# Two residual blocks with adaptive modulation on one core: engines in program order, one weight chunk per step, evacuations and attention heads as chains of tasks

## The chip, the cores and the metric

The kernel runs on one core of a Trainium2 chip. The metric is device time in microseconds (us), from the first to the last instruction of the program, as the runs give it; lower is better. Time before: 2207.31 us, the median of three runs (2190.99, 2207.31, 2212.43). TensorE (PE) multiplies, VectorE (DVE) and ScalarE (ACT) do the elementwise work, GpSimd (POOL) raises the few norm factors to their power, and SyncE (SP) issues every DMA. SBUF is the on-chip memory, PSUM the memory that PE writes.

## The reference

256 tokens of width 2048 in float32 pass four layers, and every projection is a product with a weight matrix that is used once.

```python
# first block: pooling layer, then dilated attention
hdn = rmsnorm(x, norm_a); u, gate = split(hdn @ w_in_a)                  # 2048 -> 2 x 2048
y = einsum('bsgc,gcd->bsgd', multiscale_causal_pool(u), w_grp_a) * scale_a
x = x + (y * silu(gate)) @ w_out_a
kv_in = rmsnorm(x, norm_kv); k = apply_rope(kv_in @ w_k); v = kv_in @ w_v
proj = rmsnorm(x, norm_b) @ w_in_b          # 3 groups of queries (16 heads of 128) and a gate
# 3 dilated causal windows, merged by softmax over their log-denominators
x = x + (merged * silu(gate)) @ w_out_b
x = rmsnorm(x, norm_f)
# second block: gMLP layer, then latent attention
shift, scale, gate = split(silu(c) @ ada_w[i] + ada_b[i])                # for each layer i, 2048 -> 3 x 2048
h = rms_norm(x, norm_g[i]) * (1 + scale) + shift
u, v, z = split(h @ a_w_in)                                              # 2048 -> 3 x 4096
v = layer_norm(gelu(v), a_ln_g, a_ln_b)
x = x + gate * ((gelu(u) * (tril(w_s) @ v + b_s) * silu(z)) @ a_w_out)
kv_shift, kv_scale = split(silu(c) @ kv_ada_w + kv_ada_b)                # 2048 -> 2 x 2048
# keys, values and queries through ranks of 512, 16 causal heads, gated by silu(z)
x = x + gate * (y @ b_w_out)
```

## The kernel before, in words

**Weights.** Every weight matrix is streamed once. A *chunk* is [128, 2 k-tiles, 512 columns], 512 KB of float32. SP loads it into a buffer `wraw` (L118, tag `wraw`, five buffers), ACT rounds it to a high part `wh` (L119), DVE subtracts what is left into `wl` (L125), and PE does three products per k-tile and tile of 128 tokens (L133 high by high, L134 high by low, L135 low by high): 12 matmuls of 512 columns for a chunk. There are 697 chunks. One chunk is called a *step* below. A block is 8 steps (2048 rows) or 2 steps (512 rows) that accumulate 512 output columns.

**Adaptive modulation ("ada").** The eight vectors that silu(c) makes (three for each layer of the second block, two for its keys) take 256 *parts*: a DMA of 512 KB into `araw` (L233) and one DVE instruction that multiplies and sums (L234). `araw` shares the five buffers of `wraw`. The generator `ada_all` emits a part's DMA and its DVE instruction together; `tick()` (L259) takes RATES[i] parts for each step (0.4, 0.25, 0.4, 0.4, 0.4, 0.57, 0.4, by stage), and `need()` takes what is still missing.

**Order.** The code writes each block's products, then its evacuation, then attention; a scheduler orders the instructions of each engine before the program is built, and moves the transposes of evacuations behind the products of the next chunks (DEFER = 96, L30, L194). On the chip each engine goes through its own list in order, and waits in place where something is not there yet.

**Stages by step:** pooling layer (u, ga, grp) 0 to 79; its output projection (oa) 80 to 111; keys (k) and values (v) 112 to 175; queries and gates of the dilated attention (q, gb) 176 to 303, with four heads worked at a time after each gate block; output projection (ob) 304 to 335; gMLP v (gv) to 399; u (gu), z (gz) and output projection (go), in two halves, to 591; the latent attention (cq, z, ukv, uq, o) to 696. Where a layer needs whole rows of what the one before it makes (ob3 to gv0, go13 to cq), `crossing()` interleaves the last projection with the first two of the next.

Of the kernel before, what the change touches and what calls it, by code (L numbers as in the profile page):

```python
# [10 lines left out]
F32 = mybir.dt.float32  # L11
# [9 lines left out]
T = 2  # L21
# [8 lines left out]
DEFER = 96  # L30
RATES = (0.4, 0.25, 0.4, 0.4, 0.4, 0.57, 0.4)
# [14 lines left out]

@with_exitstack
def tile_kernel(ctx: ExitStack, tc: tile.TileContext, A: dict, out: bass.AP):
    nc = tc.nc
# [7 lines left out]
    t2 = ctx.enter_context(tc.tile_pool(name="t2", bufs=9))  # L57
# [3 lines left out]
    sc_p = ctx.enter_context(tc.tile_pool(name="sc", bufs=1, space=PSUM))  # L61
# [51 lines left out]
    def whigh(W, k0, nk, n0, nn):  # L113
        """load weights and round them to their high part."""
        w = wp.tile([P, CK, NB], F32, tag="wraw", name=nm("wraw"), bufs=5)
        wh = wp.tile([P, CK, NB], F32R, tag="wh", name=nm("wh"))
        k = k0 % CK
        sp.dma_start(w[:, :nk, :nn], W[n0 // nn, k0 // CK, :, k:k + nk, :])  # L118
        act.activation(wh[:, :nk, :nn], w[:, :nk, :nn], AF.Copy)  # L119
        return w, wh, nk, nn  # L120

    def wlow(w, wh, nk, nn):
        """what the high part leaves."""
        wl = wp.tile([P, CK, NB], F32R, tag="wl", name=nm("wl"))
        dve.tensor_sub(wl[:, :nk, :nn], w[:, :nk, :nn], wh[:, :nk, :nn].bitcast(F32))  # L125
        return wh, wl

    def wsplit(*args):
        return wlow(*whigh(*args))
# [7 lines left out]
    class Stream:  # L137
        """Products of token rows (transposed, in two parts) with blocks of weights (W, n0, name).
        order: (block, first k tile, k tiles) of each step; token tile 1 runs `lag` steps behind tile 0."""

        def __init__(self, blocks, H, L, K, order, nn=NB, wk0=0, lag=0):
            self.blocks, self.H, self.L, self.K, self.order = blocks, H, L, K, order
            self.nn, self.wk0, self.lag = nn, wk0, lag
            self.ws = []
            self.ps = [[acc(nm(name)) for _ in range(T)] for _, _, name in blocks]
# [4 lines left out]
        def args(self, i):  # L150
            b, k0, nk = self.order[i]
            W, n0, _ = self.blocks[b]
            return W, self.wk0 + k0, nk, n0, self.nn

        def step(self, i):
            n = len(self.order)
            if len(self.ws) <= i < n:
                self.ws.append(wsplit(*self.args(i)))
            todo = [(i, j, t) for j in range(CK) for t in range(T)] if not self.lag else \
                   [(i, j, 0) for j in range(CK)] + [(i - self.lag, j, 1) for j in range(CK)]  # L160
            for ii, j, t in todo:
                if 0 <= ii < n and j < self.order[ii][2]:
                    b, k0, _ = self.order[ii]
                    mm3(self.ps[b][t], self.H, self.L, k0 + j, t, *self.ws[ii], j, self.nn,
                        k0 + j == 0, k0 + j == self.K - 1)
            if i < n:
                tick()

    def chunks(K, first=()):
        out, k = [], 0  # L170
        while k < K:
            n = first[len(out)] if len(out) < len(first) else min(CK, K - k)
            out.append((0, k, n))
            k += n
        return out

    def proj(W, hH, hL, K, n0, nn, name, wk0=0, lag=0, first=(), hook=None):
        """h @ W[wk0 * 128:, n0:n0 + nn] for both token tiles; hook(c, k0, nk) comes before chunk c."""
        st = Stream([(W, n0, name)], hH, hL, K, chunks(K, first), nn, wk0, lag)
        for i in range(len(st)):  # L180
            if hook:
                hook(i, *(st.order[i][1:] if i < len(st.order) else (K, 0)))
            st.step(i)
        return st.ps[0]

    def split_to(H, L, src):
        """H, L (float32r) from src (float32, SBUF or PSUM)."""
# [3 lines left out]
    def transpose_block(src, name):  # L191
        """[P, 512] SBUF -> PSUM [P, 4, P] (4 transposed blocks)."""
        pt = trp(nm(name))
        with tc.high_priority(offset=-DEFER):  # L194
            for j in range(4):
                pe.transpose(pt[:, j, :], src[:, j * P:(j + 1) * P], ident)
        return pt
# [5 lines left out]
    sc = const.tile([P, D], F32, name="silu_c")  # L203
    ada = {}

    def ada_init():
        sp.dma_start(sc, bcast_rows(A["c_2"][0], D))
        act.activation(sc, sc, AF.Silu)

    def store_row(src, dst, name):  # L210
        """[P, 16] transposed vector -> DRAM row."""
        pt = trp(nm(name))
        pe.transpose(pt[:16, 0, :], src, ident)
        row = T2(nm(name))
        dve.tensor_copy(row[:16, :P], pt[:16, 0, :])
        sp.dma_start(dst[0].rearrange("(k p) -> k p", p=P), row[:16, :P])
# [6 lines left out]

    def ada_vec(key, W, n0):
# [3 lines left out]
        bias = V(key + "_b")  # L228
        for j in range(16):
# [857 lines left out]
```

## Time and profile before

The profiled execution has a span of 2202.5 us; the median of the runs is 2207.3.

| Engine | busy us | share | instructions |
|---|---|---|---|
| PE | 2116.1 | 96% | 9646 |
| PE weight load | 1728.6 | 78% | 9646 |
| DVE | 1541.9 | 70% | 2317 |
| ACT | 1021.6 | 46% | 1395 |
| POOL | 38.7 | 2% | 29 |

538.27 MB are moved, a mean of 244 GB/s, and the mean granted clock of PE is 0.988 of full speed. Matmuls overlap in the pipeline and their ends are modelled, so PE's busy share is above the share in which it starts new work; the pace of PE is better read from the distance of starts.

### The profile page before, as it was taken

What the parts mean: (1) busy time and instruction counts of PE and PEld (TensorE: products, weight loads), DVE (VectorE), ACT (ScalarE), POOL (GpSimd) and SP (SyncE); (2) the same over time, 40 slices, a digit from 0 to 9 for tenths busy, and PEclk for the clock granted to TensorE, in tenths of its full rate; (3) what the DMA queues carried; (4) which work ended last, traced back from release to release, by engine and by line L of the source; (5) the groups of instructions that cost most, each with busy time, mean ns of one, the idle gap of its engine ahead of it and who ended that gap; (6) DMA issues with size and microseconds to landing.
All of it is one profiled execution on the core that took longest, in us unless ns stands there. A gap on an engine that the chain in (4) does not pass through costs nothing.

```text
span 2202.5 us, 26845 instructions
## 1 busy us (share of the span) xinstructions
PE 2116.1 (96%) x9646; PEld 1728.6 (78%) x9646; DVE 1541.9 (70%) x2317; ACT 1021.6 (46%) x1395; POOL 38.7 (2%) x29
## 2 busy tenths in 40 slices
PE   8999999999999999999999999989999899999999
PEld 6877777887878787877887778777888677878877
DVE  6566677755777777776777877777887678565654
ACT  6434444443444545444544334433444346765642
POOL 0000000000000000000000000000000000010000
PEclk9999999999999999999999999999999999999999
DMA  8767776777757575767688888889988875563344
GB/s 323 258 230 269 238 256 246 258 253 239 266 187 266 183 256 187 253 236 261 199 298 282 273 272 285 274 301 328 320 318 278 285 269 182 165 220 114 126 162 162
DMA packets 159781, 538.27 MB, mean 244 GB/s; under 512 B 17792, under 2 KB 22944, under 8 KB 159136
## 3 DMA queue, kind: packets, MB, share of 16 engines
q1 hardware_dynamic: 159648, 536.56, 71.2%
q8 instruction: 75, 1.23, 0.2%
q14 instruction: 58, 0.48, 0.1%
HBM read 525.99 MB, written 10.50 MB: 244 GB/s over the span
## 4 chain that ended last, share of the span: by engine, by line
PE 39%; DMA 33%; DVE 15%; issue 9%; ACT 1%; SPq 0%; POOL 0%; DVEq 0%; POOLq 0%; ACTq 0%
DMA araw<-in_ada_w 18%; DVE wl L125 9%; DMA araw<-in_kv_ada_w 7%; DMA wraw<-in_a_w_in 3%; PE q L135 2%; PE q L134 2%; PE q L133 2%; DVE araw L234 2%; DMA wraw<-in_a_w_out 1%; PE a1sc L484 1%; PE o L134 1%; PE o L135 1%; PE o L133 1%; DMA xb<-in_x 1%; PE go L135 1%
## 5 line engine op out<-in xcount | busy, mean ns | idle before, releaser
L119 ACT ACTIVATE wh<-wraw 128x1024 fp32r<-128x1024 f32 (+2 forms) x697 | 734.6, 1055 | 977.4 <-DMA wraw<-in_a_w_in 175.0
L125 DVE TENSOR_TENSOR wl<-wraw,wh 128x1024 fp32r<-128x1024 f32 (+2 forms) x697 | 834.5, 1213 | 196.6 <-ACT wh L119 194.2
L234 DVE CUSTOM_DVE_ANT_0 araw<-araw,silu_c,vec 128x1024 f32<-128x1024 f32 x128 | 164.2, 1283 | 175.1 <-DMA araw<-in_ada_w 141.7
L134 PE MATMUL q<-wl,hbH 128*128 128x512 f32 x384 | 153.7, 400 | 3.5 <-DVE wl L125 3.5
L135 PE MATMUL q<-wh,hbL 128*128 128x512 f32 x384 | 154.2, 401 | 0.0
L133 PE MATMUL q<-wh,hbH 128*128 128x512 f32 x384 | 152.3, 397 | 0.0
L135 PE MATMUL go<-wh,gyL 128*128 128x512 f32 x256 | 103.7, 405 | 8.4 <-DVE gyL L189 8.4
L134 PE MATMUL gu<-wl,hgH 128*128 128x512 f32 x256 | 102.5, 400 | 7.3 <-DVE wl L125 7.2
L133 PE MATMUL go<-wh,gyH 128*128 128x512 f32 x256 | 102.1, 399 | 5.1 <-ACT gyH L188 5.1
L134 PE MATMUL gz<-wl,hgH 128*128 128x512 f32 x256 | 102.1, 399 | 2.7 <-DVE wl L125 2.7
L133 PE MATMUL gu<-wh,hgH 128*128 128x512 f32 x256 | 101.9, 398 | 1.3 <-ACT wh L119 1.3
L134 PE MATMUL gv<-wl,hgH 128*128 128x512 f32 x256 | 100.7, 393 | 2.4 <-DVE wl L125 2.4
L134 PE MATMUL go<-wl,gyH 128*128 128x512 f32 x256 | 102.9, 402 | 0.0
L135 PE MATMUL gz<-wh,hgL 128*128 128x512 f32 x256 | 102.0, 399 | 0.0
L135 PE MATMUL gu<-wh,hgL 128*128 128x512 f32 x256 | 101.6, 397 | 0.0
L133 PE MATMUL gz<-wh,hgH 128*128 128x512 f32 x256 | 101.5, 397 | 0.0
L133 PE MATMUL gv<-wh,hgH 128*128 128x512 f32 x256 | 100.5, 392 | 0.6 <-ACT hgH L532 0.6
L135 PE MATMUL gv<-wh,hgL 128*128 128x512 f32 x256 | 100.2, 391 | 0.0
L134 PEld LDWEIGHTS q<-wl,hbH 128*128 128x128 f32 x384 | 72.5, 189 | 20.0 <-DVE wl L125 4.8
L135 PEld LDWEIGHTS q<-wh,hbL 128*128 128x128 f32 x384 | 72.6, 189 | 15.2
L133 PEld LDWEIGHTS q<-wh,hbH 128*128 128x128 f32 x384 | 72.5, 189 | 13.5
L234 DVE CUSTOM_DVE_ANT_0 araw<-araw,silu_c,ada_ga 128x1024 f32<-128x1024 f32 x32 | 41.1, 1284 | 51.9 <-DMA araw<-in_ada_w 51.9
(367 smaller groups left out, 4464.9 us busy)
## 6 DMA issues: line engine op xcount, KB each, us to landing
araw<-in_ada_w SPq DMA_DIRECT2D x192, 512.0 KB, 4.9
wraw<-in_a_w_in SPq DMA_DIRECT2D x192, 512.0 KB, 5.0
wraw<-in_w_in_b SPq DMA_DIRECT2D x128, 512.0 KB, 4.5
araw<-in_kv_ada_w SPq DMA_DIRECT2D x64, 512.0 KB, 4.6
wraw<-in_a_w_out SPq DMA_DIRECT2D x64, 512.0 KB, 5.6
wraw<-in_w_in_a SPq DMA_DIRECT2D x63, 512.0 KB, 4.9
wraw<-in_b_w_in SPq DMA_DIRECT2D x40, 512.0 KB, 3.6
wraw<-in_w_out_a SPq DMA_DIRECT2D x32, 512.0 KB, 4.7
```

The costliest lines, as they stand in the source:

```text
L119: act.activation(wh[:, :nk, :nn], w[:, :nk, :nn], AF.Copy)
L125: dve.tensor_sub(wl[:, :nk, :nn], w[:, :nk, :nn], wh[:, :nk, :nn].bitcast(F32))
L133: pe.matmul(p[:, :nn], hH[:, k, ts], wh[:, j, :nn], start=start, stop=False)
L134: pe.matmul(p[:, :nn], hH[:, k, ts], wl[:, j, :nn], start=False, stop=False)
L135: pe.matmul(p[:, :nn], hL[:, k, ts], wh[:, j, :nn], start=False, stop=stop)
L234: dve.tensor_tensor_reduce(out=w, in0=w, in1=sc[:, hs], scale=1.0, scalar=d[:, j:j + 1] if half else bias[:, j:j + 1], op0=OP.mult, op1=OP ...
L484: pe.matmul(psc[:, g * nk:(g + 1) * nk], qT[g][:, hh, t * P:(t + 1) * P], kT[:, h, :nk], start=True, stop=True)
```

## The change

The scheduler is switched off (`tc.manual_schedule()`), and each engine's instructions stand in the order in which the code emits them. A list PLAN holds all 697 chunks in the order of use. Each step calls `begin()`, then its 12 matmuls, then `end()`. `begin()` emits, in this order: `high` on ACT of the chunk four steps ahead (AHEAD); the tasks that are due in this step; one head that is ready, from `headq`; one PSUM fill from `trq` (transposes, mixing products), which is used one step later; `low` on DVE of the chunk four ahead; and the load of the chunk seven ahead. `end()` starts parts of ada by the stage's rate; the DMA is issued there, the DVE instruction follows two steps later. The evacuations, norms and heads are chains of such tasks with fixed distances in steps. The rates are 0.5 from the first gate block, 0.3 (oa), 0.5 (k), 0.7 (v), 0.5 and then 0.15, 0.15, 0 and 0.2 (attention), 0.3 and 0 (ob), 0.78 (gv), 0.5 (gu), 0.68 (gz), 0.74 (go), 0 after that. The order of blocks in the first attention changes (L1: gb2 and gb3 come last, heads are spread over the query blocks), as does that of the second one (L3); the first two blocks of `w_out_b` and of `w_out2` run as a pair. Sixteen heads of the first attention scale their output on ACT (32 instructions) and multiply by the gate in 8 DVE instructions of 128x512, where 32 DVE instructions did both. `t2` has 11 buffers for 9. The work of PE, the bytes and the five `wraw` buffers stay.

```diff
-DEFER = 96
-RATES = (0.4, 0.25, 0.4, 0.4, 0.4, 0.57, 0.4)
+AHEAD = 4
+FETCH = 3
...
+    ctx.enter_context(tc.manual_schedule())
...
-    t2 = ctx.enter_context(tc.tile_pool(name="t2", bufs=9))
+    t2 = ctx.enter_context(tc.tile_pool(name="t2", bufs=11))
...
+    L1 = [(0, 0), (1, 0), (2, 0), (3, 0), (0, 1), (1, 1), (2, 1), (3, 1), (0, 2), (1, 2), (2, 2),
+          (0, 3), (1, 3), (2, 3), (3, 2), (3, 3)]
...
+    def through(d, name, fill, use):
+
+        def go():
+            pt = trp(nm(name))
+            fill(pt)
+            after(1, lambda: use(pt))
+        if d:
+            after(d, lambda: trq.append(go))
+        else:
+            trq.append(go)
...
+        while clk["hi"] < min(n, c + clk["ahead"] + 1) and len(lows) < 2:
+            high(clk["hi"])
+            lows.append(clk["hi"])
+            clk["hi"] += 1
+        for fn in tasks.pop(clk["s"], ()):
+            fn()
+        if headq and headq[0][0] <= clk["s"] and ready.issuperset(headq[0][1]) and clk["s"] >= clk["head"] + headq[0][2]:
+            clk["head"] = clk["s"]
+            headq.pop(0)[3]()
+        if trq:
+            trq.pop(0)()
+        for i in lows:
+            low(i)
+        m = 0
+        while clk["dma"] < min(n, c + clk["ahead"] + 1 + FETCH) and m < 2:
+            fetch(clk["dma"])
+            clk["dma"] += 1
+            m += 1
+
+    def end():
+        clk["due"] += clk["rate"]
+        while clk["due"] >= 1:
+            clk["due"] -= 1
+            next(ada_gen, None)
...
-        for j in range(16):
-            for half in range(2):
-                hs = slice(half * 1024, (half + 1) * 1024)
-                w = wp.tile([P, CK * NB], F32, tag="wraw", name=nm("araw"), bufs=5)
-                sp.dma_start(w, W[n0 // P + j, half])
-                dve.tensor_tensor_reduce(out=w, in0=w, in1=sc[:, hs], scale=1.0,
+
+        def part(j, half):
+            w = wp.tile([P, CK * NB], F32, tag="wraw", name=nm("araw"), bufs=5)
+            sp.dma_start(w, W[n0 // P + j, half])
+
+            def mul():
+                dve.tensor_tensor_reduce(out=w, in0=w, in1=sc[:, half * 1024:(half + 1) * 1024], scale=1.0,
+                                         scalar=d[:, j:j + 1] if half else bias[:, j:j + 1],
+                                         op0=OP.mult, op1=OP.add, accum_out=d[:, j:j + 1])
...
+            after(2, mul)
...
+        def first():
+            score(0)
+            after(1, lambda: top(0))
+            after(2, lambda: expo(0))
+            when(2, [(("q", g, hq), 1) for g in range(3)], second)
+
+        def second():
+            score(1)
+            after_each(1, lambda: top(1), lambda: (expo(1), add(0)), lambda: add(1))
+            through(4, "a1et", etr, ecopy)
+        headq.append((clk["s"] + d, [(("q", g, hq), 0) for g in range(3)], 3, first))
...
+                clk["rate"] = (0.15, 0.15, 0.0, 0.2)[hq]
...
+    clk["rate"] = 0.78
...
+        clk["rate"] = 0.5
...
+        clk["rate"] = 0.68
...
+        clk["rate"] = 0.74
```

How this moves instructions is seen in three places. The first is SP's list in the gv stage, which holds nothing but loads; `wraw` is a chunk of weights, `araw` a part of ada, and the numbers tell tiles apart. Before:

```order
L233 DMA araw_8597<-in_kv_ada_w 128x1024
L118 DMA wraw_8606<-in_a_w_in 128x1024
L118 DMA wraw_8624<-in_a_w_in 128x1024
L233 DMA araw_8642<-in_kv_ada_w 128x1024
L118 DMA wraw_8645<-in_a_w_in 128x1024
L233 DMA araw_8663<-in_kv_ada_w 128x1024
```

and of the change:

```order
L230 DMA wraw_8662<-in_a_w_in 128x1024
L407 DMA araw_8676<-in_kv_ada_w 128x1024
L230 DMA wraw_8682<-in_a_w_in 128x1024
L407 DMA araw_8696<-in_kv_ada_w 128x1024
L230 DMA wraw_8703<-in_a_w_in 128x1024
L407 DMA araw_8717<-in_kv_ada_w 128x1024
L230 DMA wraw_8724<-in_a_w_in 128x1024
```

Before, one or two chunks stand between two parts; now parts and chunks mostly alternate. The second place is DVE's list for the same loads: `wl` reads a chunk of weights and L234 (L410 in the change) a part, and each of these reads frees one of the five buffers. Before:

```order
L125 TENSOR_TENSOR wl_8565<-wraw_8561,wh_8562 128x1024
L234 ISA araw_8597,ada_kvsh<-araw_8597,silu_c,vec 128x1024
L234 ISA ada_kvsh 128x1
L125 TENSOR_TENSOR wl_8583<-wraw_8579,wh_8580 128x1024
L125 TENSOR_TENSOR wl_8610<-wraw_8606,wh_8607 128x1024
L234 ISA araw_8642,ada_kvsh<-araw_8642,silu_c,ada_kvsh 128x1024
```

and of the change:

```order
L252 TENSOR_TENSOR wl_8680<-wraw_8622,wh_8678 128x1024
L410 ISA araw_8676,ada_kvsh<-araw_8676,silu_c,vec 128x1024
L410 ISA ada_kvsh 128x1
L252 TENSOR_TENSOR wl_8701<-wraw_8643,wh_8698 128x1024
L410 ISA araw_8696,ada_kvsh<-araw_8696,silu_c,ada_kvsh 128x1024
L410 ISA ada_kvsh 128x1
L252 TENSOR_TENSOR wl_8722<-wraw_8662,wh_8719 128x1024
L410 ISA araw_8717,ada_kvsh<-araw_8717,silu_c,vec 128x1024
```

Before, three reads stand between the read that frees a buffer for `araw_8642` (that of `wraw_8561`, after which four loads are left unread) and its own; now two stand between that for `araw_8717` (of `wraw_8643`) and its own. The third place is PE's list where the first attention starts its first head; `a1sc` are the scores of a head, L484 (L674 in the change), with 128 keys for the first tile of tokens and 256 for the second. Before:

```order
L135 MATMUL gb_833_4402<-wh_4539,hbL 128x512
L484 MATMUL a1sc_4560<-kT,qT_4015 128x128
L484 MATMUL a1sc_4560<-kT,qT_4195 128x128
L484 MATMUL a1sc_4560<-kT,qT_4376 128x128
L133 MATMUL q_1_901_4718<-wh_4721,hbH 128x512
L134 MATMUL q_1_901_4718<-wl_4724,hbH 128x512
L135 MATMUL q_1_901_4718<-wh_4721,hbL 128x512
L133 MATMUL q_1_902_4719<-wh_4721,hbH 128x512
L484 MATMUL a1sc_4572<-kT,qT_4015 128x256
```

and of the change:

```order
L295 MATMUL gb_869_4488<-wh_4455,hbL 128x512
L674 MATMUL a1sc_4578<-kT,qT_4107 128x128
L674 MATMUL a1sc_4578<-kT,qT_4290 128x128
L674 MATMUL a1sc_4578<-kT,qT_4473 128x128
L293 MATMUL gb_868_4487<-wh_4474,hbH 128x512
L294 MATMUL gb_868_4487<-wl_4483,hbH 128x512
L295 MATMUL gb_868_4487<-wh_4474,hbL 128x512
```

Before, the scores of the second tile come four products after those of the first; now they come 24 products after them, two steps.

## Rows read from the trace of the kernel before

**Rows 1.** Page, part 1: engine, busy us, share of the span, instructions.

```profile
PE 2116.1 (96%) x9646; PEld 1728.6 (78%) x9646; DVE 1541.9 (70%) x2317; ACT 1021.6 (46%) x1395; POOL 38.7 (2%) x29
```

**Rows 2.** Page, part 4: chain that ended last, by engine and by line.

```profile
PE 39%; DMA 33%; DVE 15%; issue 9%; ACT 1%; SPq 0%; POOL 0%; DVEq 0%; POOLq 0%; ACTq 0%
DMA araw<-in_ada_w 18%; DVE wl L125 9%; DMA araw<-in_kv_ada_w 7%; DMA wraw<-in_a_w_in 3%; PE q L135 2%; PE q L134 2%; PE q L133 2%; DVE araw L234 2%; DMA wraw<-in_a_w_out 1%; PE a1sc L484 1%; PE o L134 1%; PE o L135 1%; PE o L133 1%; DMA xb<-in_x 1%; PE go L135 1%
```

**Rows 3.** Windows by stretch, B to F: us, busy us per engine, clock, DMA.

```profile
57.00:539.00 482.00, 464.99 (x2065) 381.10 (x2064) 315.82 (x382) 206.34 (x235) 1.07 (x1) 0.98 0.73 250
539.00:972.20 433.20, 419.18 (x2001) 342.87 (x2000) 321.09 (x565) 200.51 (x257) 2.01 (x1) 0.99 0.67 228
972.20:1113.70 141.50, 137.46 (x614) 112.44 (x614) 101.10 (x144) 72.58 (x110) 3.11 (x4) 0.99 0.73 244
1113.70:1788.50 674.80, 647.63 (x2833) 527.30 (x2833) 508.29 (x653) 273.59 (x295) 1.59 (x1) 0.98 0.85 293
1788.50:2202.50 414.00, 397.36 (x1930) 324.79 (x1928) 259.31 (x531) 231.15 (x447) 29.99 (x17) 0.99 0.50 166
```

**Rows 4.** Windows of L133 alone (four matmuls a step), stretches C and E.

```profile
539.00:972.20 433.20, 203.17 (x512) 96.61 (x512) 0.99 0.67 228
1113.70:1788.50 674.80, 355.22 (x896) 170.42 (x897) 0.98 0.85 293
```

**Rows 5.** Timeline, PE, dense products: start us, duration us; first and last of 42.

```profile
591.64 0.39 PE L134 MATMUL gb<-wl,hbH 128*128 128x512 f32 x1
...
600.95 0.39 PE L133 MATMUL gb<-wh,hbH 128*128 128x512 f32 x1
```

**Rows 6.** Waits of DVE in stretch E: us in total, times, longest.

```profile
DVE araw L234 <- DMA araw<-in_ada_w: 80.8, 50, 4.6
DVE araw L234 <- DMA araw<-in_kv_ada_w: 44.4, 26, 3.1
DVE wl L125 <- ACT wh L119: 27.1, 23, 5.2
```

**Rows 7.** Waits of DVE in stretch C.

```profile
DVE araw L234 <- DMA araw<-in_ada_w: 44.3, 21, 3.9
DVE wl L125 <- ACT wh L119: 31.2, 33, 2.5
DVE araw L234 <- DMA araw<-in_kv_ada_w: 20.6, 9, 3.7
```

**Rows 8.** Waits of DVE in stretch B.

```profile
DVE araw L234 <- DMA araw<-in_ada_w: 129.2, 47, 4.7
```

**Rows 9.** Tile araw, whole program: from issue to landing.

```profile
DMA to landing us min/median/max: 3.3/4.8/9.4
```

**Rows 10.** Timeline in gz, DVE and SP's queue; idle before in brackets.

```profile
1418.92 1.28 DVE L234 CUSTOM_DVE_ANT_0 araw<-araw,silu_c,vec 128x1024 f32<-128x1024 f32 x1 [3.55 <-DMA araw<-in_ada_w]
1420.13 2.36 DVE L125 TENSOR_TENSOR wl<-wraw,wh 128x1024 fp32r<-128x1024 f32 x2
1420.24 0.33 SPq L233 DMA_DIRECT2D araw<-in_ada_w  x1
...
1423.79 1.28 DVE L234 CUSTOM_DVE_ANT_0 araw<-araw,silu_c,ada_sh 128x1024 f32<-128x1024 f32 x1 [1.31 <-DMA araw<-in_ada_w]
```

**Rows 11.** Timeline, PE in the first attention: heads between products.

```profile
622.80 0.59 PE L484 MATMUL a1sc<-kT,qT 128*128 128x256 f32 x2
623.23 0.27 PE L448 MATMUL a1et<-ident,a1sm 128*128 128x128 f32 x1
623.34 0.27 PE L449 MATMUL a1et<-ident,a1sm 128*128 128x128 f32 x1
623.45 1.03 PE L484 MATMUL a1sc<-kT,qT 128*128 128x256 f32 x4
```

**Rows 12.** Waits of PE in stretch C.

```profile
PE a1sc L484 <- DVE a1sms L426: 12.8, 4, 5.5
```

**Rows 13.** Page, part 5, one of the costliest groups: busy us, mean ns, idle before.

```profile
L119 ACT ACTIVATE wh<-wraw 128x1024 fp32r<-128x1024 f32 (+2 forms) x697 | 734.6, 1055 | 977.4 <-DMA wraw<-in_a_w_in 175.0
```

More of the change, by code (lines that the diff above doesn't have):

```diff
@@ L128, in wsplit, with after, when @@
-    def wsplit(*args):
-        return wlow(*whigh(*args))
+    clk = {"s": 0, "c": 0, "dma": 0, "hi": 0, "ahead": AHEAD, "rate": 0.0, "due": 0.0, "head": 0}
+    tasks = {}
+    raws, parts = {}, {}
+    def after(d, fn):
+        tasks.setdefault(clk["s"] + d, []).append(fn)
+    trq, headq = [], []
+    ready = set()
+    def when(d, keys, fn):
+        def go():
+            if ready.issuperset(keys):
+                fn()
+            else:
+                after(1, go)
+        after(d, go)
@@ L391, in rope_evac @@
+    after(4, inv_b)
+    after(6, rope_inv)
     def rope_evac(p, t, tab, name):
@@ L402, in rope_evac, with rope_block, go, out @@
         return a
-    pace["rate"] = RATES[2]
+    def rope_block(ps, name, key, dst):
+        for t in range(T):
+            def go(t=t):
+                a = rope_evac(ps[t], t, rope, name)
+                def out(pt):
+                    act.activation(dst(t), pt, AF.Copy)
+                    ready.add((key, t))
+                tr_then(2, a, name + "tr", out)
+            after(1 + t, go)
+    clk["rate"] = 0.5
     kT = B16(F32, "kT")
@@ L573, in crossing @@
             if i == last + s1.lag:
[L574 to L582 removed]
+                fin(0, s1.ps[0])
+        fin(1, s1.ps[1])
+        clk["ahead"] = AHEAD
     x3d = dram.tile([S, D], F32, name="x3d")
@@ new lines, in tile_kernel, with ob_gmod @@
+    obs = []
+    def ob_gmod():
+        need("sh0", "sc0")
+        gm0.append(gmod("sc0", "norm_g0"))
+    after(12, ob_gmod)
+    after(11, lambda: obs.append(Ob(0, 0)))
+    after(14, lambda: obs.append(Ob(1, 0)))
+    proj2(["ob0", "ob1"], mH, mL, 12, lambda b, ps: obs[b].whole(ps))
+    clk["rate"] = 0.3
+    ob = Ob(2, 4)
+    ob.whole(proj(mH, mL, KT, "ob2"))
+    clk["rate"] = 0.0
+    ob = Ob(3, 6)
+    hH, hL = B16(F32R, "hgH"), B16(F32R, "hgL")
+    vg = [big.tile([P, GW], F32, tag="b16", name=f"vg{t}") for t in range(T)]
@@ L959, in tile_kernel @@
[L959 to L981 removed]
+            as_.append(a)
@@ new lines, in ntr, with out, rtr, fill @@
+        def ntr(t):
+            def out(pt):
+                act.activation(qs_[hq][0][:, :, t * P:(t + 1) * P], pt, AF.Copy, scale=V("g_qn"))
+                ready.add(("qn", hq, t))
+            tr_then(0, ns[t], "q2tr", out)
+        def rtr(t):
+            def fill(pr):
+                for h in range(4):
+                    pe.transpose(pr[:64, h, :], as_[t][:, h * 64:(h + 1) * 64], ident)
+            def out(pr):
+                act.activation(qs_[hq][1][:, :, t * P:(t + 1) * P], pr[:64], AF.Copy)
+                ready.add(("qr", hq, t))
+            through(0, "q2rt", fill, out)
@@ new lines, in tile_kernel @@
+    need("ga1")
+    o2s = [O2(0, 10), O2(1, 12)]
+    proj2(["o20", "o21"], oH, oL, 12, lambda b, ps: o2s[b].whole(ps))
+    o2 = O2(2, 4)
+    o2.whole(proj(oH, oL, KT, "o22"))
+    o2 = O2(3, 4)
+    clk["ahead"] = LAG
+    s = Stream(["o23"], oH, oL, KT, chunks(KT), lag=LAG)
+    for i in range(len(s)):
+        s.step(i)
+        if i == len(s.order) - 1:
+            o2.evac(s.ps[0][0], 0)
+    assert not trq
+    for k in sorted(tasks):
+        clk["s"] = k
+        for fn in tasks.pop(k):
+            fn()
@@ L984, in _constants @@
+    o2.evac(s.ps[0][1], 1)
+    assert not tasks and clk["c"] == len(PLAN)
 def _constants():
```

1307 lines of the change are left out of this document (776 added, 531 removed).

## The prediction, made before the change was run

> **What bounds the kernel now.** I read the page from the outside in. PE is busy for 96% of the span [rows 1], but the chain that ended last has only 39% of PE in it: DMA holds 33%, most of it landings of `araw` (18% and 7%), and DVE 15% [rows 2]. Busy PE isn't PE at its pace, since ends are modelled. The pace shows in a dense stretch: 42 products of 512 columns start within 9.31 us [rows 5], 0.227 apart, so a step of 12 is 2.72 us. I then cut the span where the steps 16, 176, 304, 352 and 576 begin, into stretches B to F [rows 3] (A, the first 57 us, is left alone: its first chunk and its x bound it in both).
>
> E holds 896 / 4 = 224 steps [rows 4], which at 2.72 us are 609 us; its other 145 PE instructions, at about 0.12 us each (transposes start 0.11 apart [rows 11]), add 17. PE needs 627 us there and the stretch takes 674.8 [rows 3]. What fills it is DVE: 508.3 us busy [rows 3], 125.2 us waiting for parts of ada to land (76 waits) and 27.1 us for ACT [rows 6], together 661, and what is left (14) goes to small waits. Nothing of weight waits for PE. So from gv to go DVE sets the time, and three quarters of the time in which it doesn't compute (125 of 166.5 us) are landings. C is the same: 321.1 busy, 64.9 landings, 31.2 for ACT [rows 3, 7] are 417 of 433.2. In B 129.2 us are landings [rows 8].
>
> Why a landing is waited for is seen in gz [rows 10]. DVE's product at 1418.92 frees a buffer, SP issues the next part at 1420.24, two `wl` take 2.36 us, and then the next product stands at the head of DVE's queue until 1423.79. The landing took 3.6 us there and takes 4.8 as a median [rows 9]. Everything behind waits too: `wl`, evacuations, and in the attention the score masks, for which PE waited 12.8 us in 4 waits [rows 12].
>
> **What the change does to this.** PE's work and the bytes stay, so the terms are waits. Five buffers serve chunks and parts in both versions, and a part's load can start only when at most four loads are unread. So the DVE work between the read that frees its buffer and its own read is fixed by DVE's and SP's lists. I counted it for every part in both, at DVE's pace in the trace (some 1.2 us for a `wl` and for a part, start to start [rows 10]). In the lists shown above it is a part and two `wl`, 3.5 us, before, and a part and one `wl`, 2.3 us, in the change. Call the *shortfall* 4.8 us less that work, where it is positive. The number of parts moves as well, by the rates.
>
> - **E, gv to go.** Parts 126 before, 146 after (rates 0.78, 0.5, 0.68, 0.74 for 0.57). With under 3.8 us of work between: 83 of 126 before, 128 of 146 after. Shortfalls sum to 165 us before, of which DVE really waited 125.2 [rows 6], that is 0.76 (one wait covers part of the next landing). After, they sum to 288; 0.76 of that is 219 us. DVE then needs 508.3 + 20 x 1.28 (the added parts [rows 10], 25.6) + 219 = 753 us, +78, with the waits for ACT and the norm's loads taken as gone. Lower bound: waits per part stay at 125.2 / 126 = 0.99 us, 146 x 0.99 = 145, in all 679, +4. Upper bound: every shortfall is waited for, 822, +147. I take +62, nearer the first figure, since the count of close parts is in the lists and only the landing can give: a longer stretch carries its bytes at a lower rate (293 GB/s now [rows 3]), which shortens landings a little. What covers nothing here: the `low` four steps ahead is a stock of 11 us, spent once.
> - **C, first attention.** Parts 52 to 23; shortfall 102 to 32, so landings 64.9 to 21 us. DVE: 321.1 - 29 x 1.28 + 21 = 305 and some 30 for ACT, no longer the bound. PE is: 128 x 2.72 = 348, plus 16 heads at some 2.9 us (6 scores at 0.215, 6 at half of it, 3 transposes at 0.11, 6 products at 0.11 [rows 11]), 46, plus 128 transposes, 15: 410. I keep 5 us of PE's 14 of idle time for scores that wait for the softmax [rows 12]. 415, -18. Bounds: 0 to -23. The 16 heads' scaling on ACT is hidden, ACT is busy for 201 of 433 us [rows 3]; without that cover 32 instructions of 128 columns cost between an eighth and a half of 1.055 us each [rows 13], 4 to 17 us.
> - **B, pooling to values.** Parts 60 to 78 (rates 0.5, 0.3, 0.5, 0.7), 18 x 1.28 = 23 us more work; shortfall 145 to 153, landings 129.2 to 136. DVE 315.8 + 23 + 136 = 475, with small waits about the 482 of now; PE needs 160 x 2.72 + 145 x 0.12 = 452. 0, bounds -20 and +30.
> - **D, ob and the crossing.** The chain through the norm (reduce, power on POOL, row on PE, splits) stands as it was; pairing ob0 and ob1 moves its waits. 0, bounds -6 and +6.
> - **F, rest.** 7 parts leave, heads are spread over 11 blocks, POOL makes one factor of 16 columns for two of 8. PE shows 414.0 - 397.4 = 16.6 us of idle [rows 3]; I take it as gained, -16. Bounds: 0, and -30 for idle that modelled ends hide. A head's scores, tops and copies now stand at fixed places in PE's and DVE's lists; if a predecessor is late, products queue behind it.
>
> Sum: 2202.5 + 62 - 18 + 0 + 0 - 16 = 2230.5 us for a profiled execution. The median of the runs stands 4.8 above the profiled one, so 2235.
>
> **The rivals.** *Landings are hidden (faster).* Parts and chunks alternate and each is issued at a fixed place, so fewer loads may be in flight at once; a landing alone takes 3.3 us, the shortest row [rows 9]. At 3.3 E's shortfalls are 117, 0.76 of it 89; DVE needs 623 us there, PE 627, so E takes some 639 (-36). B gains its 20, C and F as above: 2202.5 - 36 - 20 - 18 - 16 = 2112, or 2117 as a median. It decides from a landing of about 3.8 us downwards (where DVE's sum in E falls to the 675 of now). Against it: the median is 4.8 with fewer parts. [...]
>
> *Waits per part stay as they are.* One wait in a close pair covers the other's landing, so closeness costs nothing more: E at +4, the rest as forecast, 2202.5 + 4 - 18 - 16 = 2172.5, median 2177. For it: 0.76 is already under 1. Against it: waits in B, where more parts are close (44 of 61 under 2.6 us), are 129.2 / 60 = 2.2 us per part [rows 8], not 0.99.
>
> *The fixed order of PE adds stalls (slower still).* Some 260 fills stand at fixed places, and the scheduler's freedom to have put them behind what was ready is gone. At 0.1 us each this is 26 us on top of my sum, 2261. Against it: a fill is used a step after it is written, and its input is made one or two steps (2.7 to 5.4 us) before.
>
> *The change doesn't do what it says.* The lists show the order as described; under 0.02, and I leave it out.
>
> **How the numbers follow.** My case 0.50, with a range of its own from 2195 to 2262 (E between +22 and +89); fixed-order stalls 0.17; waits per part unchanged 0.20; landings hidden 0.13. About 1% (22 us) is what a measurement of this kernel can tell from no change, so faster is below 2185 and slower above 2229. My case puts 0.30 of its 0.50 above 2229 and the rest between; stalls put 0.15 above; unchanged waits put 0.14 below 2185 and 0.06 within; hidden landings all below. Faster 0.27, same 0.28, slower 0.45. The range leaves out the lower part of the hidden landings and the upper part of the stalls, about 0.1 on either side: 2135 to 2275.
>
> **What would show it.** Right: in the profile after, E (from the third gv block to the third block of go's second half) is longer than 674.8 us with DVE waiting some 200 us for `araw` there, and landings near 4.8; C is near 415 us with under 30 us of such waits, and PE's dense starts there; F is near 398. E near 640 with landings under 4 us would make the first rival right, E near 680 with about 1 us of wait per part the second. Many short waits of PE for `tr` and `sc` tiles, or a granted clock well under 0.988 over a stretch, would make the third right. My step most likely to fail is that the landing keeps its median: the shortfall counts every tenth of it 128 times in E.

## The result, and the profile after

The changed kernel takes 2311.98 us (median of four runs, 2305.68 to 2315.03) where the kernel before takes 2204.38 beside it: 1.0485 times as long, 95% interval 1.0444 to 1.0527. Slower was forecast, at 2235 us with a range up to 2275; the loss is about four times as large as forecast and lies outside the range.

The page of the profile after, part 1 (engine, busy us, share of the span, instructions), answers to [rows 1]:

```profile
PE 2144.7 (93%) x9646; PEld 1742.9 (75%) x9646; DVE 1554.8 (67%) x2253; ACT 1016.0 (44%) x1382; POOL 31.0 (1%) x25
```

PE runs the same 9646 instructions; the span of the profiled execution grew from 2202.5 to 2313.3 us. The same cuts as in [rows 3], at the starts of steps 16, 176, 304, 352 and 576 (windows of the kernel after: us, busy us of PE, weight load, DVE, ACT, POOL, clock, DMA share, GB/s):

```profile
55.80:530.10 474.30, 462.79 (x2080) 379.43 (x2081) 337.90 (x420) 207.83 (x239) 0.70 (x1) 1.00 0.81 272
530.10:962.50 432.40, 417.33 (x1995) 346.81 (x1994) 287.70 (x465) 207.31 (x289) 0.00 (x0) 0.99 0.58 190
962.50:1116.60 154.10, 140.37 (x622) 113.67 (x621) 100.84 (x142) 73.36 (x111) 4.12 (x5) 0.97 0.66 223
1116.60:1879.60 763.00, 672.60 (x2834) 536.52 (x2833) 536.63 (x684) 272.64 (x295) 0.70 (x1) 0.96 0.81 274
1879.60:2313.30 433.70, 405.60 (x1929) 329.59 (x1927) 256.78 (x504) 222.09 (x400) 24.57 (x13) 0.97 0.46 151
```

E (gv to go) is the loss: 763.0 after 674.8. C (first attention) stayed at 432.4, D (ob and its crossing) grew by 12.6 and F (second crossing and the rest) by 19.7. In E the clock was granted at 0.96 for 0.98 and the memory carried its bytes at a lower rate than before, 274 GB/s for 293. DVE's busy time grew by 28 us, of which the 20 added parts are 26. What grew most is DVE's waiting for parts (waits of DVE in E after: us in total, times, longest), which answers to [rows 6]:

```profile
DVE araw L410 <- DMA araw<-in_ada_w: 130.8, 78, 5.3
DVE araw L410 <- DMA araw<-in_kv_ada_w: 70.6, 45, 3.3
DVE gyL L356 <- ACT gyH L355: 9.4, 9, 2.8
DVE wl L252 <- ACT wh L242: 7.4, 8, 2.1
```

These are 201.4 us of landings in 123 waits, where it was 125.2 in 76 before. So the 88 us more in E are 28 of DVE's work and 76 of landings, less 16 that DVE waits less for all else (25 us for 41). The pattern repeats for whole blocks (timeline of the kernel after in gu, DVE and SP's queue: start us, us, operation, idle before in brackets):

```profile
1297.71 2.35 DVE L252 TENSOR_TENSOR wl<-wraw,wh 128x1024 fp32r<-128x1024 f32 x2
1297.83 0.33 SPq L407 DMA_DIRECT2D araw<-in_kv_ada_w  x1
...
1302.45 1.28 DVE L410 CUSTOM_DVE_ANT_0 araw<-araw,silu_c,ada_kvsc 128x1024 f32<-128x1024 f32 x1 [2.38 <-DMA araw<-in_kv_ada_w]
...
1303.66 2.35 DVE L252 TENSOR_TENSOR wl<-wraw,wh 128x1024 fp32r<-128x1024 f32 x2
1303.77 0.33 SPq L407 DMA_DIRECT2D araw<-in_kv_ada_w  x1
...
1308.15 1.28 DVE L410 CUSTOM_DVE_ANT_0 araw<-araw,silu_c,vec 128x1024 f32<-128x1024 f32 x1 [2.14 <-DMA araw<-in_kv_ada_w]
```

A product frees the buffer, the next part is issued 0.1 us later, two `wl` cover 2.4 us of a landing of 4.6, and DVE stands. A landing of 4.6 us is the median of all parts (tile `araw` after, beside [rows 9]; it is also that of E alone):

```profile
DMA to landing us min/median/max: 3.3/4.6/9.7
```

PE, which waited 27 us in E before, now waits 90 us there, for what is queued behind that. The longest waits of PE in E, before:

```profile
PE go L135 <- DVE gyL L189: 8.4, 4, 3.0
PE gu L134 <- DVE wl L125: 7.2, 5, 2.1
```

and after:

```profile
PE gytr L369 <- DVE gz L1085: 27.1, 7, 8.8
PE gu L294 <- DVE wl L252: 22.6, 15, 5.4
PE go L294 <- DVE wl L252: 15.5, 11, 3.1
PE gv L294 <- DVE wl L252: 12.5, 14, 2.0
```

In C the landings fell as forecast, from 64.9 to 18.6 us, and still PE waited there (waits of PE in C after, beside [rows 12]):

```profile
PE qrtr L369 <- DVE qr L617: 9.4, 3, 6.4
PE a1sc L674 <- ACT qT L627: 2.4, 2, 1.2
PE a1sc L674 <- DVE a1s L682: 2.1, 2, 1.5
```

Where in C this was is seen if it is cut once more, at step 200 (window of steps 176 to 199 of the kernel after, and the waits of DVE in it):

```profile
530.10:613.60 83.50, 74.11 (x325) 60.54 (x324) 58.05 (x80) 32.41 (x35) 0.00 (x0) 0.94 0.74 245
```

```profile
DVE araw L410 <- DMA araw<-in_ada_w: 18.6, 8, 3.4
DVE wl L252 <- ACT wh L242: 6.5, 4, 1.8
```

All of C's landings are waited for in its first 24 steps, where parts are still started at the rate of 0.5. There DVE's busy time and its waits (58.1 + 18.6 + 6.5 us) fill the 83.5 us: DVE is the bound, and PE's whole wait for `qr` lies there.

### The profile page after: what moved, and what is told of

Same layout as the page of the kernel before. It is cut to its first block, busy times and chain, and to the rows that moved or that the text cites. A ratio compares the mean times of both kernels' runs of the same rounds, so it can differ in the third digit from the quotient of the medians.

```text
span 2313.3 us, 26922 instructions
## 1 busy us (share of the span) xinstructions
PE 2144.7 (93%) x9646; PEld 1742.9 (75%) x9646; DVE 1554.8 (67%) x2253; ACT 1016.0 (44%) x1382; POOL 31.0 (1%) x25
## 5 line engine op out<-in xcount | busy, mean ns | idle before, releaser
L410 DVE CUSTOM_DVE_ANT_0 araw<-araw,silu_c,vec 128x1024 f32<-128x1024 f32 x128 | 164.3, 1283 | 175.5 <-DMA araw<-in_ada_w 131.0
L294 PEld LDWEIGHTS gu<-wl,hgH 128*128 128x128 f32 x256 | 49.3, 193 | 39.9 <-DVE wl L252 30.1
```

The lines of the kernel that those rows point to most:

```text
L294: pe.matmul(p[:, :nn], hH[:, k, ts], wl[:, j, :nn], start=False, stop=False)
L410: dve.tensor_tensor_reduce(out=w, in0=w, in1=sc[:, half * 1024:(half + 1) * 1024], scale=1.0, scalar=d[:, j:j + 1] if half else bias[:, j: ...
```

## The experiments

The theory from the prediction is called theory A in the expectations below: parts of ada stand too near to their own loads on DVE. Its rivals are PE's fixed order (theory B), and too few buffers whatever is read first (theory C). The columns A to F of the table are something else, the stretches of the text above, cut at the same steps in every kernel, in us of the profiled execution. The last column is the median of four or more executions for the first two rows and the kernel with 4 steps, and a single execution for the others; where an interval is given below, there were four. B and C repeat within 0.1 us in kernels whose edits leave them alone, but E lies between 662.5 and 668.9 for 4 steps with edits that lie outside it, so differences of a few us in E are not read:

| Kernel | A | B | C | D | E | F | whole, us |
|---|---|---|---|---|---|---|---|
| before | 57.0 | 482.0 | 433.2 | 141.5 | 674.8 | 414.0 | 2204 |
| after (product 2 steps after the load) | 55.8 | 474.3 | 432.4 | 154.1 | 763.0 | 433.7 | 2312 |
| 3 steps | 57.9 | 457.7 | 418.2 | 153.0 | 677.3 | 433.9 | 2200 |
| 4 steps | 55.9 | 457.8 | 416.5 | 152.6 | 666.6 | 436.0 | 2185 |
| after, no parts | 56.2 | 457.7 | 417.6 | 153.0 | 633.1 | 433.8 | 2153 |
| before, no parts | 56.3 | 461.7 | 414.9 | 142.6 | 633.7 | 406.1 | 2117 |
| after, even rates | 58.1 | 473.5 | 433.1 | 153.6 | 722.9 | 433.7 | 2277 |
| 4 steps, even rates | 56.2 | 457.7 | 422.0 | 153.0 | 664.7 | 432.5 | 2188 |
| 2 steps, 7 buffers | 56.9 | 457.6 | 419.1 | 156.9 | 646.7 | 438.0 | 2177 |
| 4 steps, rows behind products | 57.9 | 457.7 | 416.4 | 150.8 | 662.5 | 432.4 | 2179 |
| 4 steps, low parts later | 59.3 | 457.7 | 416.5 | 152.0 | 664.0 | 433.3 | 2185 |
| 4 steps, pieces in three steps | 56.3 | 457.7 | 416.5 | 149.7 | 668.9 | 419.2 | 2170 |
| the same, statistics earlier | 55.8 | 457.7 | 416.4 | 145.2 | 667.7 | 417.9 | 2163 |

### One line: when a part is read

```diff
-            after(2, mul)
+            after(4, mul)
```

> The changed kernel with one line altered: the DVE instruction of a part of ada comes 4 steps after its load is issued instead of 2. By the lists of the built program the DVE work between the read that frees a part's buffer and the part's own read grows from a mean of 2.9 us to 5.8 in the gv to go stretch (148 parts), and for the chunks of weights it shrinks from 7.8 to 6.7. Theory A (the landings set that stretch): DVE's waits for araw there fall from 201 us to under 50, the stretch from 763 us to 655 to 690, and the whole from 2312 to about 2210. Theory B (PE's fixed order sets it: transposes and fills that stand ahead of products): the waits fall, but the stretch stays above 740 and the whole above 2285. Theory C (five buffers are short whatever is read first): the wait moves to the chunks, ACT waits for wraw some 100 us more, and the stretch stays near 730, the whole near 2280.

Measured: 2184.7 us, 0.9904 of the kernel before (0.9876 to 0.9932), 127 us less than the change. Theory A forecast about 2210. In the whole program DVE's waits for parts are down to nothing (waits before the tile `araw`, whole program, kernel with 4 steps):

```profile
  DMA araw<-in_ada_w: 2.3, 3
  DMA araw<-in_kv_ada_w: 0.3, 1
```

though a landing's median is longer there, 5.1 us, than in the kernels before and after, 4.8 and 4.6:

```profile
DMA to landing us min/median/max: 3.4/5.1/9.6
```

E is 666.6, with 148 parts, and C 416.5 (window of E with 4 steps):

```profile
1082.70:1749.30 666.60, 643.38 (x2834) 527.21 (x2833) 532.04 (x679) 271.63 (x294) 1.56 (x1) 0.99 0.89 311
```

DVE now waits for ACT's `wh` instead (82.9 us in E, where it was 7.4), but that is time it has to spare: PE's waits for `wl` in E fell from 52 to 15 us. ACT's waits for chunks to land, 288 us in E of the changed kernel, are 277, so the wait didn't move to the chunks: theory C falls as the cause of what this edit gained. Theory B falls for E, since PE's list kept its order. PE's waits in E for `gytr` fell from 27.1 to 1.5 us: they were what the parts had made late.

> The same with 3 steps instead of 2 or 4. Mean DVE work between is 4.3 us in the gv to go stretch, the sum of shortfalls (4.8 us less that work, where positive) 115 us there after 288 at 2 steps and 10 at 4. Theory A: DVE's waits for araw there fall from 201 to about 80 us, the stretch to some 680 to 700 us, the whole to about 2230, between the changed kernel and the one with 4 steps. Theory B: no change, above 2285.

Measured: 2199.82 us, E 677.3, waits for parts 75.0 there (waits of DVE in E, 3 steps):

```profile
DVE araw L410 <- DMA araw<-in_ada_w: 46.4, 40, 4.6
DVE araw L410 <- DMA araw<-in_kv_ada_w: 28.6, 35, 2.2
```

The sums of shortfalls, 288, 115 and 10 us for 2, 3 and 4 steps, gave waits of 201, 75 and about 3. The waits were forecast well (80), the time less so (2200 for 2230): once PE leads again, 75 us of DVE's waits cost only 11 of E. That the stock of finished chunks takes up the rest is my reading; no run varies that stock alone.

### Without any parts

```diff
-            w = wp.tile([P, CK * NB], F32, tag="wraw", name=nm("araw"), bufs=5)
-            sp.dma_start(w, W[n0 // P + j, half])
...
-                dve.tensor_tensor_reduce(out=w, in0=w, in1=sc[:, half * 1024:(half + 1) * 1024], scale=1.0,
...
+                    dve.tensor_copy(d, bias)
```

(in the changed kernel; the same is left out of the kernel before)

> The changed kernel without the adaptive modulation's loads and products: each of the eight vectors is a copy of its bias, nothing else is left out. So no part is loaded, waited for or computed, and what is left is the order itself. Theory A: gv to go falls from 763 to 640 to 665 us (PE needs 627), pooling to values from 474 to about 455, the first attention from 432 to about 425, the whole to about 2185. Theory B: gv to go stays above 720, the whole above 2260.

> The kernel before without the adaptive modulation's loads and products, vectors are copies of their biases. Theory A: gv to go falls from 675 to about 635 us, the first attention from 433 to about 412, pooling to values from 482 to about 456, the whole from 2202 to about 2113. What the changed kernel without it takes above this one is the price of the fixed order by itself: from the traces 35 to 70 us, in the two crossings, the attentions and the transposes. Theory B: the difference is 100 us or more, all of the loss.

Measured: 2153.18 us, below the 2185 expected, and 2117.06 us. In E both are PE's pace and equal (windows of E without parts, kernel after and kernel before):

```profile
1084.50:1717.60 633.10, 633.10 (x2834) 524.58 (x2833) 363.58 (x393) 273.08 (x295) 0.70 (x1) 1.00 0.64 206
```

```profile
1075.50:1709.20 633.70, 633.68 (x2833) 523.57 (x2832) 363.23 (x397) 275.63 (x295) 1.60 (x1) 1.00 0.64 206
```

So the new order by itself costs nothing in E, gains 4 us in B, and costs 36 us in all: 3 in C, 10 in D and 28 in F, where the crossings are.

### Number or nearness

```diff
-    clk["rate"] = 0.78
+    clk["rate"] = 0.58
...
-                clk["rate"] = (0.15, 0.15, 0.0, 0.2)[hq]
+                clk["rate"] = (0.4, 0.4, 0.1, 0.2)[hq]
```

> The changed kernel with the parts of ada spread about as before: a rate of 0.58 in all of gv to go (129 parts there by the lists, for 146) and 0.4, 0.4, 0.1, 0.2 in the first attention (42 parts for 23); the product still comes 2 steps after the load is issued. It tells the number of parts in the last stretch from their nearness. Theory A (nearness, each near part costs DVE its wait): shortfalls in gv to go fall from 288 to 241 us, of which 0.70 was waited in the changed kernel, so 168 us of waits after 201; with 17 fewer parts of 1.28 us the stretch is some 705 to 715 us after 763, the first attention rises from 432 to about 440, the whole is about 2265. Rival (the 20 added parts are the loss): the stretch returns to about 680 and the whole to about 2235.

Measured: 2276.58 us, E 722.9, above both readings, nearest to theory A's. With 129 parts in E, where the kernel before has 126, E is 48 us above it; as the order costs nothing in E without parts, that is nearness. The 17 parts more that the change has there are the other 40, half of them DVE's work (17 x 1.28 = 22 us) and half waits (201.4 - 181.6 = 20 us). The waits behind them (waits of DVE in E, even rates) are 181.6 us, not the 168 expected:

```profile
DVE araw L410 <- DMA araw<-in_ada_w: 136.1, 77, 6.4
DVE araw L410 <- DMA araw<-in_kv_ada_w: 45.5, 30, 2.8
```

> The kernel with 4 steps and the even rates of the earlier run (129 parts in gv to go, 42 in the first attention). That stretch takes 666.6 us with 148 parts and 633.1 without any, so 33.5 us still hang on the parts. If each costs the same, 0.23 us, the stretch falls by only 4 us, to 662, and the whole to about 2181. If it is DVE's or DMA's load near its limit (278 GB/s and 80% of DVE's time there), the last parts cost most: about 645 to 650, and the first attention, with 18 more parts, stays within 4 us of 416.5; the whole about 2168.

Measured: 2187.84 us, E 664.7 for 666.6, C 422.0 for 416.5: once parts are read in time their number hardly counts, and moving them gives nothing. The second reading of that expectation fell (the memory carries 311 GB/s in E with 4 steps, not the 278 named there), and the whole was not the 2181 of the first either.

### Buffers

```diff
-AHEAD = 4
+AHEAD = 3
...
-    wp = ctx.enter_context(tc.tile_pool(name="wp", bufs=5))
+    wp = ctx.enter_context(tc.tile_pool(name="wp", bufs=4))
...
-        w = wp.tile([P, CK * NB], F32, tag="wraw", name=nm("wraw"), bufs=5)
+        w = wp.tile([P, CK * NB], F32, tag="wraw", name=nm("wraw"), bufs=7)
```

(and the same 7 for `araw`)

> The changed kernel with its product 2 steps after the load as it is, but chunks rounded three steps ahead instead of four, and the memory so freed given to the loads: 7 buffers for chunks and parts instead of 5, 4 instead of 5 for high and low parts. DVE work between is 5.8 us for parts in gv to go, 10.9 for chunks (7.8 in the changed kernel, 6.7 with the product at 4 steps). Theory A (a landing needs buffers or distance, either will do): waits for araw go below 20 us, gv to go to 660 or less, the whole to about 2180 or less. If the stock of finished chunks matters more, the whole stays above 2215.

Measured: 2176.82 us, E 646.7, waits for parts 20.3 us there. Distance in DVE's list or buffers, either will do for the parts, and buffers give the chunks their distance as well. ACT's waits for chunks to land in E show it, with 4 steps and five buffers:

```profile
ACT wh L242 <- DMA wraw<-in_a_w_in: 203.0, 111, 7.4
ACT wh L242 <- DMA wraw<-in_a_w_out: 73.8, 33, 5.1
```

and with 2 steps and seven:

```profile
ACT wh L242 <- DMA wraw<-in_a_w_out: 11.4, 4, 5.6
ACT wh L242 <- DMA wraw<-in_a_w_in: 9.8, 2, 8.3
```

So theory C holds for most of what 4 steps leave in E: 666.6 became 646.7, with 633.1 for no parts at all.

### The crossings

In the changed kernel the step in which the crossing turns over takes 15.0 us in both, where the kernel before has 8.3 and 7.0; and the steps 591 to 599 of the second take 2.7 to 8.6 us where before all take 2.7.

```diff
-            if i == n0 + 1:
-                rbs.append(stats(0, pb[:, 0:P]))
-                evac_tr(0)
             s0.step(i)
+        rbs.append(stats(0, pb[:, 0:P]))
+        evac_tr(0)
```

(and the second tile's behind the first step of the next layer)

> The kernel with 4 steps, and in both crossings PE's two instructions that need the norm of a token tile (the row of factors and the transposes) stand behind the next products instead of ahead of them, and DVE's statistics with them. If PE's place for them is what made the crossing's longest step 15.0 us (7.0 to 8.3 before), that step falls to about 9 in both crossings, the stretches with ob and with the rest lose some 5 to 6 us each, the whole goes from 2185 to about 2174. If the short stock of chunks (two steps ahead in a crossing, four elsewhere) made it, nothing changes by more than 2 us.

Measured: 2179.43 us. The long step falls to 10.0 and 9.8, but the two after it rise, in the first crossing from 4.3 and 3.5 to 6.3 and 5.3: D gains 1.8, F 3.6. The place of PE's instructions was mostly not the cause.

```diff
+            if late:
+                after(2, lows)
+            else:
+                lows()
```

> The kernel with 4 steps, and in both crossings the four joint pieces of the split input (and the four of the keys' input) make their low part one step later than their high part, so that DVE doesn't wait for ACT in between. In the second crossing the steps 591 to 598 take 3.2 to 5.9 us, 38 in all for 8, where the kernel before takes 2.7 each; DVE has there some 2.8 us of work and 1.05 of waits for ACT a step. If these waits are the loss, the steps fall to about 2.9 and the last stretch loses some 8 us, the first crossing some 3, the whole goes to about 2174. If it is DVE's work, the steps stay above 3.4 and the whole above 2181.

Measured: 2184.58 us, the steps 591 to 598 still take 3.3 to 4.5 us each (31 us in all with 4 steps alone, not 38). So the loss was not DVE's waits for the high part, but not the sum of work on DVE either, which was busy for 22.5 of 30.2 us there. The timeline of this kernel shows a ring (DVE and ACT in the second crossing, without the low part `h2L` that stands between):

```profile
1811.14 0.75 DVE L786 TENSOR_TENSOR hx<-z,inv_row 128x256 f32<-128x256 f32 x2
1811.92 0.91 ACT L790 ACTIVATE h2H<-hx,ada_sh 128x256 fp32r<-128x256 f32 x2 [1.96 <-DVE hx L786]
1812.74 1.04 ACT L242 ACTIVATE wh<-wraw 128x1024 fp32r<-128x1024 f32 x1
1813.82 1.22 DVE L252 TENSOR_TENSOR wl<-wraw,wh 128x1024 fp32r<-128x1024 f32 x1 [1.14 <-ACT wh L242]
1814.96 1.41 DVE L786 TENSOR_TENSOR hx<-zk,inv_row 128x256 f32<-128x256 f32 x4
```

From `hx` to `hx` 3.82 us: ACT rounds the chunk only behind the high part, that waits for `hx`, and `hx` stands behind the chunk's `wl`. Neither engine is full, and each waits for the other once a step.

```diff
+            if late:
+                after_each(1, highs, lows)
```

> The kernel with 4 steps, and the late pieces of the crossings go in three steps: the product with the row of factors, a step later the high part (behind the rounding of a chunk in ACT's list), another step later the low part. With only the low part moved the steps 591 to 598 stayed at 3.2 to 4.5 us. If they are set by a ring of the two lists (hx on DVE 0.75 to 0.9 us until ACT can start, high part 0.9, rounding of the chunk 1.06, wl 1.14, then the next hx, about 3.8 us a step), then this breaks it: the steps fall to about 2.8, the last stretch from 436 to about 427, the first crossing loses 2 to 3, the whole goes from 2185 to about 2175. If it is the sum of work on one engine, the steps stay above 3.4 and the whole above 2181.

Measured: 2169.99 us. Steps 591 to 598 take 2.7 us each, step 599 4.4 for 8.6, F 419.2 after 436.0, D 149.7 after 152.6: the ring was the loss in these steps, and more of it than expected. They give back 14 us; 2 of the 17 in F lie in step 576, which the edit doesn't touch. The first two edits of this section together:

> The last two together on the kernel with 4 steps. If the two losses lie in different steps they add: some 20 to 22 us, to about 2163 us, 0.982 of the kernel before. If one hides behind the other, about 2172.

Measured: 2178.69 us, 0.9887 (0.9862 to 0.9912). They don't add, since the low parts alone gave nothing.

> The kernel with 4 steps and the crossings' pieces in three steps, and in both crossings DVE's statistics of the first token tile stand straight behind its evacuation, ahead of the next chunk's wl, while PE's rows and transposes stand behind the products that follow. In the changed kernel these statistics stood for 2 us behind a wl that waited for ACT. If that place is what is left of the crossing's long step, the first three steps of the crossing go from 23.7 us to about 19 in each, the whole from 2170 to about 2160. If the chain through the norm sets them whatever the order (as the rows behind the products gave nothing), they stay at 22 to 24 and the whole at 2166 to 2172.

Measured: 2162.59 us. The long step is 7.2 and 7.7 us, the two after it 6.5 and 5.1, and 6.3 and 6.3: the first three steps go from 23.3 and 23.7 to 18.8 and 20.3, D from 149.7 to 145.2, F only from 419.2 to 417.9, where a fourth step takes 3.6. So in the first crossing the place of the statistics, behind a `wl` that waits for ACT, was worth nearly what was expected. This edit moves PE's rows as well; in the first kernel of the next section, which has the rows, the pieces and the even rates, D is 148.7, so some 3.5 of the 4.5 us are the statistics. F is 4 us above the kernel before, which has 7 parts there, and 12 above that kernel without parts: this remainder is open.

### Versions that beat both

> 4 steps, even rates, the rows behind the products, and the pieces of the crossings in three steps. Gains of its parts if they add: 10 us from the pieces, 5 from the rows, 4 to 17 from the rates, on 2185 us: 2153 to 2166, 0.977 to 0.983 of the kernel before. If the two edits in the crossings hide each other, 2165 to 2175.

Measured: 2168.0 us, 0.9831 (0.9804 to 0.9857). Its D of 148.7 and F of 422.3 stand beside 149.7 and 419.2 with the pieces alone, and its C is 422.0 for 416.5: the even rates gave nothing, the rows next to nothing.

> The crossings' pieces in three steps, the product 3 steps after the load, and chunks three steps ahead with 7 buffers for the loads. With four steps and 5 buffers gv to go takes 667 to 669 us, 34 above the kernel without parts. If those 34 us are loads that come late because five buffers hold too few (ACT waits for wraw), the stretch falls to about 642, the crossings lose 2 to 3 us each with the smaller stock, and the whole is about 2150, 0.975 of the kernel before. If they are the memory's rate (311 GB/s there), the stretch stays above 655 and the whole at about 2165.

Measured: 2157.85 us, 0.9797 (0.9755 to 0.9838), E 641.9. So 25 to 27 of the 34 to 36 us were late loads for want of buffers, and not the memory, which carried 323 GB/s there and 311 with 4 steps and five buffers (window of E):

```profile
1086.50:1728.40 641.90, 636.70 (x2835) 526.43 (x2834) 533.31 (x680) 273.87 (x295) 1.62 (x1) 0.99 0.91 323
```

F is 429.2 there and 419.2 with five buffers, D 153.9 and 149.7. The likely reason is the smaller stock of finished chunks (three steps for four), which costs more than expected in the crossings; the stock and the buffers were not run apart.

> The last two together. If both hold, about 2142 us; if only the buffers do, about 2150.

Measured, in a single execution: 2151.68 us, near its second reading. E is 640.8, D 149.6 and F 426.2: the statistics gave 4 us in D and 3 in F, and the crossings stay the loss.

## Why the prediction was wrong

**What bounds the kernel: right.** From gv to go DVE and the landings set the time. Taking the parts out moved E from 674.8 to 633.7 in the kernel before; reading them two steps later moved it from 763.0 to 666.6 in the change.

**E: right mechanism, a term put at nothing, 26 us.** The forecast was +62; measured +88.2. The terms: DVE busy 536.6 us (534 forecast); landings 201.4 (219 from the rows, 203 with the 16 us that I took off because a longer stretch should shorten landings); and 25 us of other waits of DVE (`gyL` 9.4, `wl` 7.4, the norm's loads 6.4, small ones), which I had "taken as gone" without a reason. The discount was right: the median landing in E fell from 5.0 to 4.6 us, where the second is the line shown after the change and the first is this (tile `araw` in E, before):

```profile
DMA to landing us min/median/max: 3.4/5.0/9.4
```

So the miss in E is the other waits, 25 us, and 1 us between the first two terms.

**C: a step failed, 17 us.** I had DVE "no longer the bound" at 305 us and PE at 415. DVE was busy 287.7 and waited 18.6 for parts, near the forecast, and C took 432.4. With the same list and parts read in time it takes 416.5, without parts 417.6. So some 23 parts cost 16 us, nearly all of their waits. The step that failed is the sum over all of C: it set the waits against DVE's spare time in the whole stretch, but they all lie in the first 24 steps, where DVE has none. Those steps take 83.5 us, and 70.3 with 4 steps (window of steps 176 to 199 there):

```profile
513.70:584.00 70.30, 70.30 (x326) 58.30 (x325) 55.27 (x78) 30.41 (x33) 0.00 (x0) 1.00 0.77 267
```

That PE had to stand behind DVE's late queries is in its waits (`qrtr` 9.4 us in 3 waits), and with 4 steps that wait is gone.

**D and F: two steps failed, 13 and 36 us.** I wrote that the chain through the norm "stood as it was" and took PE's 16 us of idle time in F as gained. D grew by 12.6, F by 19.7; without parts the two kernels differ by 10 and 28 there, so it is order and not parts (the kernel before has 7 parts in F, the change none). In F some 14 us of it are the ring between ACT and DVE. In D the ring is 2.9 and the statistics behind a `wl`, with PE's rows, 4.5. The rest is open. The wait of PE for the first row of factors is in the rows after (D; 2.2 us in one wait before):

```profile
PE inv_row L775 <- POOL s L880: 9.0, 2, 5.1
```

**B: nothing forecast, 7.7 gained.** Landings fell to 115.5 us where 136 were forecast; with them gone B is 457.8, near PE's 452.

These make the miss: E 26, C 17, D 13, F 36, less 8 in B and 1 at the start, 83 us of a span forecast at 2230.5 and measured at 2313.3.

**The rivals.** Hidden landings: no, the median was 4.6, and DVE waited 346.9 us for parts in all, where it was 340.9 in the kernel before. In nine of the kernels with parts the shortest landing was 3.3 to 3.4 us and the median 4.5 to 5.2, so no median reached the 3.8 us from which this rival decides. Waits per part unchanged: no, 0.99 us became 201.4 / 146 = 1.38 in E. Fixed-order stalls: I priced them at 26 us spread over 260 fills of PE, 0.1 us each by an estimate of mine that no run shows. The order does cost 36 us without parts, but nearly all in the two crossings, in part by the lists of DVE and ACT, while in E it costs nothing. So this rival came true beside my case and by another mechanism in part. Its time, 2261, already held my sum, and 2312 lies 51 us beyond it. The signs that I gave for it misled: PE did wait for transposes (`gytr` 27.1 us) and its clock was 0.96 in E, but with the same list of PE and parts read 4 steps after their loads the wait is 1.5 us and the clock 0.99.

## What to carry to other kernels

In an in-order list, compare for each load the work between the read that frees its buffer and its own read with a landing in the trace; when loads of two kinds share buffers, what one kind gains the other gives up in part (from 2 to 4 steps the parts went from a mean of 2.9 to 5.8 us of work between, the chunks from 7.8 to 6.7), and it pays to give the near kind some of the far kind's distance (here one number, 127 us). When an order is written by hand, follow the items of one step around all engines: a ring such as `hx`, high part, rounding, `wl` sets the step (3.82 us from `hx` to `hx` here) though no engine is full (DVE was busy for 22.5 of 30.2 us). And a stretch's sum per engine bounds the time from below only: cut it where the rates change, for the 18.6 us of waits in 24 steps of C cost 13 us there, though DVE had time to spare in the other 104.

## What the runs showed of the hardware

In the kernel with seven buffers and pieces in three steps the memory carried 323 GB/s over 642 us with DMA at 0.91, while that stretch took 9 us more than without parts. The median landing of the whole program rose only from 4.6 to 5.1 and 5.2 us between the changed kernel (274 GB/s in E) and the kernels with 311 and 320 GB/s: parts were late in the kernel with the shorter landings and the lower rate, so it was not the load of the memory that made them late.

The granted clock was lower where PE waited more: 0.96 in E of the changed kernel, where PE waited 90 us, 0.99 with 4 steps (23 us), and 1.00 without parts, where no wait of PE is listed. These are means over the whole stretch. In one place in C of the changed kernel PE stood for 6.4 us until 542.12, and the products behind that start 0.43 us apart, then 0.23 (timeline of PE):

```profile
542.12 1.09 PE L369 MATMUL qrtr<-ident,qr 128*128 128x128 f32 x4 [6.39 <-DVE qr L617]
...
543.43 0.63 PE L294 MATMUL q<-wl,hbH 128*128 128x512 f32 x1
543.86 0.63 PE L295 MATMUL q<-wh,hbL 128*128 128x512 f32 x1
...
546.44 0.40 PE L293 MATMUL q<-wh,hbH 128*128 128x512 f32 x1
546.67 0.39 PE L294 MATMUL q<-wl,hbH 128*128 128x512 f32 x1
```

with the clock (the third number from the end, in windows of the same stretch) at 0.51 and then at 1.00:

```profile
541.50:546.00 4.50, 3.88 (x12) 3.26 (x13) 4.47 (x7) 0.00 (x0) 0.00 (x0) 0.51 0.67 219
546.00:560.00 14.00, 14.00 (x65) 11.59 (x64) 9.52 (x12) 6.28 (x7) 0.00 (x0) 1.00 0.77 258
```
